# Where the depthwise convolution's taps, its tail and two sets of transposes stand in a two-layer hybrid encoder kernel

## The chip, the cores and the metric

The kernel runs on one core of a Trainium2 chip. The metric is the device time of one execution in microseconds (us). Five engines work from queues of their own, each strictly in the order of its program: PE (TensorE, matrix multiplies), DVE (VectorE), ACT (ScalarE), POOL (GpSimd) and SP, which issues the DMAs here. They wait for each other through semaphores.

## The reference, cut to what matters

Two layers are computed on x of 1 x 1024 x 1024, float32:

```python
for l in range(DEPTH):                       # 2 layers
    h = rms_norm(x, norm_mix[l]); z = h @ w_in[l]
    (q_a, k_a, v_a, q_h, i_h, f_fw, f_bw, g_h, a_c, g_c) = split(z)
    o_att = block_attention(rope(rms_norm(q_a)), rope(rms_norm(k_a)), v_a)   # 8 query, 2 key/value heads of 64
    o_hg  = hgrn2_bidirectional(q_h, i_h, f_fw, f_bw, g_h, ...)              # gated recurrence, 4 heads of 64
    u     = a_c * sigmoid(g_c)
    y     = depthwise_conv(u, w_dw) + b_dw                                   # 31 taps, 256 channels
    o_cv  = silu(layer_norm(y, ln_g, ln_b))
    x = x + concat([o_att, o_hg, o_cv]) @ w_out[l]
    x = x + square(relu(rms_norm(x) @ w_mlp_in[l])) @ w_mlp_out[l]
```

## The kernel before, in words

Channels lie on the 128 partitions and the 1024 positions on the free axis. A float32 product is made of three passes over operands split into a high and a low part (`xs`, `whi`, `wlo`), so one projection of 128 columns is 48 matmuls 128x512 at L223 (`dense_steps`), into two banks of PSUM (the tile `S2`). The projections of a layer go in a fixed order of columns: convolution inputs, the first half of the HGRN heads (`Hgrn(0)`), v, k and the four q columns, then the second half (`Hgrn(1)`). In the traces, buffer numbers are left out, so `S2` reads `S`, `x8` reads `x` and `m4` reads `m`.

What stands around the change, in the program's order, per layer:

- `conv_in(0)`, `conv_in(1)` make u for two halves of the channels. `conv(i)` is a generator: a first multiply, then 30 taps, each one DVE instruction over up to 1024 elements (L352), with a `yield` behind each. `conv_tail` is the layer norm and the swish behind both: POOL sums the halves, PE makes sums over channels (`tok_sums`, L162), ACT widens them (L168), PE flips them (`flip`, L178), DVE subtracts (L379); then squares, second sums, `rstd` (eleven small DVE steps on 128x8, L151 to L156), again widen and flip, DVE multiplies (L394), POOL scales (L397), ACT takes the sigmoid (L398), POOL multiplies (L399), and SP stores into `mixd` (L400). `cg` runs through conv(0), conv(1) and the tail.
- `Hgrn(ls)` makes five projections, evacuates each on DVE (`evac`, L322), and turns the value tile `iv` with eight PE transposes into `vt` (L442, L443).
- `h0.core()` is the recurrence of the first half: `near`, then seven levels of DVE and POOL multiplies of `X` by `T` (L525, L526), with scores on PE between (L494), masked into `A` on DVE (L501, L505). Between its steps the loop advances `qg` (the projections of v, k and q with their norms and rotations) and `cg`.
- `att_query(0)`, `keys(0)`, `h1 = Hgrn(1, ...)`: within it `mid()` computes the attention scores of units 0 and 1 (L745) ahead of the last projection, `iv`. Then `drain(cg)`, `keys(1)`, and the attention loop over 64 units: scores, P on DVE (L756), exponent on ACT (L759), its reciprocal on DVE (L760), normalisation on POOL (L761), transposes on PE (`att_flip`, L782), copies on ACT and DVE (L786, L787), values on PE (L803). The queries of units 4 to 7 are loaded by SP (L729), copied on ACT (L733) and split on DVE (L735).

The order on each engine is not the source's order. A list scheduler of the framework takes the instructions as written and starts one where it believes its inputs to be ready; a tap written late may so stand early. Tiles of a tag share a fixed number of buffers: `e` (`pse`) two banks, `c` two, `S2` two pairs, `tmp` four.

The loop and its end before:

```python
for _ in h0.core():
    for g in (qg, cg, qg, cg):
        next(g, None)
drain(qg)
while not ys[1:]:
    next(cg)
```

Of the kernel before, what the change touches and what calls it, by code (L numbers as in the profile page):

```python
# [45 lines left out]
def tile_hybrid_trunk(  # L46
# [59 lines left out]
    def tmp(shape=(P, L), dt=F32):  # L106
        return sp_.t(shape, "tmp", bufs=4, dt=dt)
# [179 lines left out]
    for l in range(DEPTH):  # L287
# [38 lines left out]
        def conv_in(i):  # L326
# [10 lines left out]
            nc.gpsimd.tensor_tensor(u, a, s, op=ALU.mult)  # L337
            us.append(u)

        def conv(i):  # L340
            u = us[i]
            y = x8()
            wof = PAR["cw"][0] + i * CK
            nc.vector.tensor_scalar(
                y, u, par[:, l, wof + CPAD : wof + CPAD + 1], pv(l, "cb", i), op0=ALU.mult, op1=ALU.add
            )
            for tap in range(CK):
                d = tap - CPAD
                if d == 0:
                    continue  # L350
                lo, hi = max(0, -d), min(L, L - d)
                nc.vector.scalar_tensor_tensor(  # L352
                    y[:, lo:hi], u[:, lo + d : hi + d], par[:, l, wof + tap : wof + tap + 1], y[:, lo:hi],
                    op0=ALU.mult, op1=ALU.add,
                )
                yield
            ys.append(y)

# [7 lines left out]
        def conv_tail(ys):  # L366
# [28 lines left out]
            for i, y in enumerate(ys):  # L395
# [3 lines left out]
                nc.gpsimd.tensor_tensor(s, s, y, op=ALU.mult)  # L399
                nc.sync.dma_start(mixd[2 + i], s)  # L400

        class Hgrn:
            def __init__(self, ls, mid=lambda: None):
                self.ls = ls

                X = self.X = hg.t([P, 4, L], "X")
                T = self.T = hg.t([P, 2, L], "T")
                vt = self.vt = hg.t([P, 8, P], "vt")
                hq = self.hq = hg.t([P, L], "m4", bufs=5)
                evac(ztile(6 + ls), hq)  # L410
                for d, kslot, qslot in ((0, 0, 2), (1, 3, 1)):
                    zt = tmp()
                    evac(ztile(10 + 2 * d + ls), zt)
                    if ls == 1:
                        next(cg, None)
                    nc.scalar.activation(T[:, d], zt, AF.Sigmoid)
                    nc.scalar.activation(X[:, kslot], zt, AF.Sigmoid, scale=-1.0)
                    om = oml[:, l, d, ls : ls + 1]
                    nc.scalar.activation(T[:, d], T[:, d], AF.Identity, scale=om, bias=lbt[:, l, d, ls : ls + 1])
                    nc.scalar.activation(X[:, kslot], X[:, kslot], AF.Copy, scale=om)  # L420
                    nc.vector.tensor_tensor(X[:, qslot], hq, T[:, d], op=ALU.mult)
                hks = self.hks = hg.t([P, L], "m4", bufs=5)
                nc.vector.tensor_tensor(hks, X[:, 0], X[:, 3], op=ALU.add)
                gl = tmp()
                evac(ztile(14 + ls), gl)
                if ls == 1:
                    next(cg, None)
                gate = tmp()
                nc.scalar.activation(gate, gl, AF.Sigmoid)
                if ls == 1:  # L430
                    nc.scalar.activation(cst.t([P, 4], "mx", bufs=4)[:, 0:1], gate[:, 0:1], AF.Exp)
                nc.gpsimd.tensor_tensor(gate, gate, gl, op=ALU.mult)
                nc.gpsimd.tensor_scalar(gate, gate, pv(l, "hn", ls), 0.0, op0=ALU.mult, op1=ALU.add)
                nc.sync.dma_start(gd[ls], gate)
                mid()
                iv = self.iv = hg.t([P, L], "m4", bufs=5)
                evac(ztile(8 + ls), iv)
                for h in range(2):
                    tpv = pse()
                    for q in range(4):  # L440
                        c = h * 4 + q
                        nc.tensor.transpose(tpv[:, q * P : (q + 1) * P], iv[:, c * P : (c + 1) * P], ident)  # L442
                    nc.scalar.activation(  # L443
                        vt[:, h * 4 : h * 4 + 4, :], tpv.rearrange("p (a b) -> p a b", a=4), AF.Copy
                    )

            def near(self):
                X, w0, iv = self.X, self.hks, self.iv
                nc.gpsimd.tensor_tensor(w0, w0, self.hq, op=ALU.mult)
                w1 = hg.t([P, L], "m4", bufs=5)  # L450
                pair = lambda t: t.rearrange("p (n h) -> p n h", h=2)
                for hf in range(2):
                    nc.vector.tensor_tensor(
                        pair(w1)[:, :, hf], pair(X[:, 1 + hf])[:, :, hf], pair(X[:, 3 - 3 * hf])[:, :, 1 - hf],
                        op=ALU.mult,
                    )
                yield
                t = tmp()
                for h in range(2):
                    sl = slice(h * 512, (h + 1) * 512)  # L460
                    d1 = pse()
                    nc.tensor.matmul(d1, same_head, w1[:, sl], start=True, stop=True)
                    for hf in range(2):
                        nc.vector.tensor_tensor(
                            pair(t[:, sl])[:, :, hf], pair(d1)[:, :, hf], pair(iv[:, sl])[:, :, 1 - hf], op=ALU.mult
                        )
                yield
                for h in range(2):
                    sl = slice(h * 512, (h + 1) * 512)
                    d0 = pse()  # L470
                    nc.tensor.matmul(d0, same_head, w0[:, sl], start=True, stop=True)
                    nc.vector.tensor_tensor(iv[:, sl], d0, iv[:, sl], op=ALU.mult)
                nc.gpsimd.tensor_tensor(iv, iv, t, op=ALU.add)
                yield

            def scores(self, lev):
                X = self.X
                s = LEVELS[lev]
                kx, qx = (hg.t([P, L], "m4", bufs=5) for _ in range(2))
                for dst, arrs in ((qx, (1, 2)), (kx, (0, 3))):  # L480
                    for hf in range(2):
                        nc.scalar.activation(
                            dst.rearrange("p (n h s) -> p n h s", h=2, s=s)[:, :, hf],
                            X[:, arrs[hf]].rearrange("p (n h s) -> p n h s", h=2, s=s)[:, :, hf],
                            AF.Copy,
                        )
                for g in range(2):
                    scs = [pse(), pse()] if g == 1 or self.ls == 1 else [psc(), psc()]
                    for q in range(4):
                        c = g * 4 + q  # L490
                        cs = slice(c * P, (c + 1) * P)
                        for hh in range(2):
                            rows = slice(64 * hh, 64 * hh + 64)
                            nc.tensor.matmul(  # L494
                                scs[hh][:, q * P : (q + 1) * P], kx[rows, cs], qx[rows, cs], start=True, stop=True
                            )
                    for hh in range(2):
                        dst = self.A[:, hh, g * 4 : g * 4 + 4, :]
                        src = scs[hh].rearrange("p (a b) -> p a b", a=4)
                        if lev == 0:  # L500
                            nc.vector.tensor_tensor(  # L501
                                dst, src, masks[:, 0].unsqueeze(1).to_broadcast([P, 4, P]), op=ALU.mult
                            )
                        else:
                            nc.vector.copy_predicated(  # L505
                                dst, masks[:, lev].unsqueeze(1).to_broadcast([P, 4, P]), src
                            )
                    yield

            def core(self):  # L510
# [3 lines left out]
                for s in (1,) + LEVELS:  # L514
# [5 lines left out]
                    for eng, d, arr, half in (  # L520
# [2 lines left out]
                        tv = Tv[:, d, :, 1 - half, 0:1].to_broadcast([P, nb, s])  # L523
                        xv = Xv[:, arr, :, half, :]
                        eng.tensor_tensor(xv, xv, tv, op=ALU.mult)  # L525
                    nc.vector.tensor_tensor(  # L526
                        Tv[:, :, :, 0, 0], Tv[:, :, :, 0, 0], Tv[:, :, :, 1, 0], op=ALU.mult
                    )
                    yield
                Tc = cst.t([P, 2, 8], "Tc", bufs=2)  # L530
                nc.vector.tensor_copy(Tc, T.rearrange("p d (n s) -> p d n s", s=P)[:, :, :, 0])
# [155 lines left out]
        def qkv():  # L687
# [5 lines left out]

            for col, part in [(5, vpart), (4, kpart)] + [(j, lambda zp, j=j: qpart(zp, j)) for j in range(4)]:
                for k, _ in enumerate(zsteps(col, lambda zp: start(part(zp)))):
                    if k == 2 and rest:
                        drain(rest.pop(0))
                    yield
            drain(rest.pop(0))

        qg = qkv()
        for _ in h0.core():
            for g in (qg, cg, qg, cg):
                next(g, None)
        drain(qg)
        while not ys[1:]:
            next(cg)

        KH, KL = [], []

# [55 lines left out]
        h1 = Hgrn(1, lambda: (att_scores(0), att_scores(1)))  # L766
        gen = h1.core()
        drain(cg)
        xsp.close()


# [513 lines left out]
```

## Time and profile before

| | |
|---|---|
| time, median of 3 runs | 2544.08 us (2543.35 to 2545.97) |
| profiled execution | 2543.87 us, its span 2541.9 us |
| PE busy | 2457.1 us, 97% |
| DVE, ACT, POOL busy | 78%, 47%, 29% |
| DVE, the 120 taps (L352) | 166.8 us, mean 1390 ns |
| chain that ended last | PE 78%, DVE 15%, ACT 3% |

The span is the time from the first to the last instruction in the trace; some 2 us of the execution lie outside of it. Layer 0's part from the convolution to the attention lies between 60 and 340 us, layer 1's between 1323 and 1600 us. A tap is written into the profile as `L352 DVE SCALAR_TENSOR_TENSOR x<-x,par,x`. A bracket behind a row of the timeline is the engine's idle time before the row and what released it.

### The profile page before, as it was taken

The page shows a single profiled execution, that of the slowest core. Times are in us where ns is not written, and L with a number is a line of the kernel's source. Part 1 is how long each engine was busy: PE and PEld are TensorE (multiplying, and loading weights), DVE is VectorE, ACT ScalarE, POOL GpSimd, SP SyncE. Part 2 cuts the span into 40 slices and gives each one's busy share as a digit, 9 for nine tenths or more (in the row PEclk, how much of TensorE's full clock was granted, in tenths as well). Part 3 has the DMA queues.
Part 4 walks back from the last instruction along what each step waited for, and adds up shares of the span by engine and source line. Part 5 has one row for each costly group of instructions (what it writes and reads, how often), then busy time and mean ns, then how long its engine had stood idle before and what let it go on. Part 6 is the DMA issues. An engine that isn't in the chain of part 4 may idle for free.

```text
span 2541.9 us, 34037 instructions
## 1 busy us (share of the span) xinstructions
PE 2457.1 (97%) x12608; PEld 2023.4 (80%) x12608; DVE 1995.0 (78%) x3051; ACT 1205.0 (47%) x1960; POOL 736.7 (29%) x463
## 2 busy tenths in 40 slices
PE   8989989999999999999999899999999999999999
PEld 7777778878788887888887777788787888878887
DVE  5998598872887778987859985898628777789876
ACT  4222478773544444443433224787635444444332
POOL 0232565433034430000123324665330354300000
PEclk9999999999999999999999999999999999999999
DMA  4101210033244448454131113000322544584542
GB/s 149 68 25 63 95 43 18 14 106 115 75 165 164 144 158 322 159 174 156 67 108 50 42 63 104 17 18 26 124 84 91 178 141 154 185 287 158 162 153 91
DMA packets 113078, 286.99 MB, mean 113 GB/s; under 512 B 11409, under 2 KB 11665, under 8 KB 112913
## 3 DMA queue, kind: packets, MB, share of 16 engines
q1 hardware_dynamic: 112912, 284.83, 32.4%
q8 instruction: 99, 1.62, 0.3%
q14 instruction: 67, 0.54, 0.1%
HBM read 197.75 MB, written 87.03 MB: 112 GB/s over the span
## 4 chain that ended last, share of the span: by engine, by line
PE 78%; DVE 15%; ACT 3%; issue 2%; POOL 2%; DMA 0%; SPq 0%; DVEq 0%; ACTq 0%; POOLq 0%
PE S L223 15%; PE S L1196 10%; PE c L995 10%; PE S L995 7%; PE e L995 7%; PE e L1196 6%; PE c L1196 6%; DVE x L352 4%; PE e L803 4%; PE c L782 3%; PE S L745 3%; PE e L494 2%; DVE P L756 1%; PE e L162 1%; PE e L583 1%
## 5 line engine op out<-in xcount | busy, mean ns | idle before, releaser
L223 PE MATMUL S<-xs,whi 128*128 128x512 f32 x1280 | 366.3, 407 | 10.6 <-ACT xs L208 9.1
L223 PEld LDWEIGHTS S<-xs,whi 128*128 128x128 f32 x1280 | 245.0, 195 | 67.5 <-ACT xs L208 9.1
L1196 PE MATMUL S<-xs,xs 128*128 128x512 f32 x816 | 201.6, 390 | 2.6 <-DVE xs L897 2.6
L223 PE MATMUL S<-xs,wlo 128*128 128x512 f32 x640 | 204.0, 399 | 0.0
L896 ACT ACTIVATE xs<-m 128x512 fp32r<-128x512 f32 x216 | 126.0, 619 | 141.6 <-DVE m L907 50.8
L761 POOL TENSOR_SCALAR P<-P,mx 128x1024 f32<-128x1024 f32 x124 | 142.6, 1150 | 164.1 <-DVE mx L760 126.2
L787 DVE TENSOR_TENSOR PT<-c,PT 128x512 fp32r<-128x512 f32 x256 | 171.1, 684 | 24.2 <-ACT PT L786 22.6
L1196 PEld LDWEIGHTS S<-xs,xs 128*128 128x128 f32 x816 | 152.8, 188 | 35.5 <-DVE xs L897 3.5
L786 ACT ACTIVATE PT<-c 128x512 fp32r<-128x512 f32 x256 | 147.5, 593 | 69.1 <-PE c L782 65.5
L199 ACT ACTIVATE whi<-raw 128x1024 fp32r<-128x1024 f32 x56 | 59.1, 1058 | 247.1 <-PE S L223 234.1
L803 PE MATMUL e<-PT,x 128*128 128x256 f32 x1024 | 172.3, 297 | 0.8 <-ACT PT L786 0.5
L756 DVE TENSOR_SCALAR_CACHE_REDUCE P<-S,nqc 128x1024 f32<-128x1024 f32 x124 | 158.5, 1278 | 14.0 <-PE S L745 8.8
L352 DVE SCALAR_TENSOR_TENSOR x<-x,par,x 128x1009 f32<-128x1009 f32 (+14 forms) x120 | 166.8, 1390 | 1.8
L782 PE MATMUL c<-cons,P 128*128 128x128 f32 x992 | 152.4, 278 | 10.5 <-POOL P L761 5.6
L897 DVE TENSOR_TENSOR xs<-m,xs 128x512 fp32r<-128x512 f32 x216 | 144.9, 694 | 22.0 <-ACT xs L896 22.0
L745 PE MATMUL S<-x,QS 128*128 128x512 f32 x480 | 154.0, 419 | 4.8 <-DVE P L756 4.5
L260 POOL TENSOR_TENSOR tmp<-tmp,tmp 128x1024 f32<-128x1024 f32 x19 | 50.6, 2662 | 360.4 <-ACT tmp L259 360.2
L759 ACT ACTIVATE P<-P,mx 128x1024 f32<-128x1024 f32 x124 | 142.4, 1149 | 24.3 <-DVE P L756 23.0
L803 PEld LDWEIGHTS e<-PT,x 128*128 128x128 f32 x1024 | 139.0, 193 | 8.5 <-ACT PT L786 2.0
L223 PEld LDWEIGHTS S<-xs,wlo 128*128 128x128 f32 x640 | 123.2, 193 | 27.1 <-issue 0.3
L782 PEld LDWEIGHTS c<-cons,P 128*128 128x128 f32 x992 | 115.3, 141 | 36.7 <-issue 10.6
L1196 PE MATMUL e<-xs,xs 128*128 128x512 f32 x552 | 140.6, 390 | 0.3 <-DVE xs L897 0.3
(310 smaller groups left out, 5639.1 us busy)
## 6 DMA issues: line engine op xcount, KB each, us to landing
m<-ad SPq DMA_DIRECT2D x104, 512.0 KB, 3.8
ad<-x SPq DMA_DIRECT2D x176, 256.0 KB, 2.2
raw<-w_in_t SPq DMA_DIRECT2D x40, 512.0 KB, 3.4
xs<-w_t SPq DMA_DIRECT2D x36, 512.0 KB, 3.7
raw<-w_t SPq DMA_DIRECT2D x36, 512.0 KB, 3.7
m<-w_t SPq DMA_DIRECT2D x32, 512.0 KB, 6.8
ad<-tmp SPq DMA_DIRECT2D x48, 256.0 KB, 2.2
x<-w_t SPq DMA_DIRECT2D x24, 512.0 KB, 4.6
```

Source lines behind the costliest of these rows:

```text
L223: nc.tensor.matmul(zp[h] if type(zp) is list else zp[:, h, :], w, xx[:, h * 512 : (h + 1) * 512], start=first, stop=last)
L352: nc.vector.scalar_tensor_tensor(y[:, lo:hi], u[:, lo + d : hi + d], par[:, l, wof + tap : wof + tap + 1], y[:, lo:hi], op0=ALU.mult, op1= ...
L745: nc.tensor.matmul(S[:, hb, :], qs, kk[:, hb * 512 : (hb + 1) * 512], start=first, stop=not first)
L756: nc.vector.tensor_scalar(Pt, S, nqc[:, j, ci : ci + 1], 3.0e38, op0=ALU.mult, op1=ALU.min, accum_out=mx[:, 1:2])
L761: nc.gpsimd.tensor_scalar(Pt, Pt, mx[:, 3:4], 0.0, op0=ALU.mult, op1=ALU.add)
L782: nc.tensor.transpose(t[:, q * P : (q + 1) * P], Pt[:, hb, q * P : (q + 1) * P], ident)
L786: nc.scalar.activation(hi, src, AF.Copy)
L787: nc.vector.tensor_tensor(lo, src, hi.bitcast(F32), op=ALU.subtract)
L803: nc.tensor.matmul(pvp[:, cs], VS[g][:, hb * 4 + kb, :], pt[:, kb, :], start=hb == 0 and n == 0, stop=hb == 1 and n == 7,)
L897: ordered("v", nc.vector.tensor_tensor(lo, src, hi.bitcast(F32), op=ALU.subtract))
L995: nc.tensor.matmul(bank, w[i][:, kt * P : (kt + 1) * P], BC[name][kt][j], start=n == 0 and name not in ("M6", "M7", "M3"), stop=n == 11, s ...
L1196: nc.tensor.matmul(banks[dt], w[i][:, dt * P : (dt + 1) * P], a[j], start=n == 0 and name not in ("M6", "M7", "M3"), stop=n == 3 * SG - 1, ...
```

## The change: what it does

1. **Taps by hand.** A helper `taps(n)` advances `cg` n steps. In `Hgrn(0)` it is called with 6, 6, 6, 6 and 5 behind the projections: 29 taps, where before none was written. In the loop of `h0.core()` one tap is written in every second step from the sixth on (12), where before two were written in every step. In `Hgrn(1)` 3, 4, 4 and 4 are written, and `drain(cg)` writes the last four taps and the whole tail behind `Hgrn(1)`. The loop that finished the taps ahead of `Hgrn(1)` is gone, so no part of the tail is written ahead of the scores of units 0 and 1 any more.
2. **A gate for the scheduler.** A tap written within the first recurrence may not be scheduled ahead of the latest masked copy (L505) or `T` product (L526): these are put into `mark`, and each tap gets an order-only dependency on the last of them. `mark` is emptied behind the recurrence and behind the tail.
3. **Two sets of transposes later.** The eight transposes of `iv` move from the end of `Hgrn` into `near`, behind its first multiplies (`turned`). In `qkv` the second part of v (its eight transposes and their split copies) is run at the seventh step of k's projection, where it was the third.

```diff
+        def after_gate(i):
+            if mark:
+                tc.add_manual_dep(i.ins, mark[-1].ins.name, mybir.DependencyInfo(
+                    mybir.DependencyClass.NoSync, mybir.DependencyReason.DATA), reason="order")
...
+        def taps(n):
+            for _ in range(n):
+                next(cg, None)
...
                 evac(ztile(6 + ls), hq)
+                taps(3 if ls else 6)
                 for d, kslot, qslot in ((0, 0, 2), (1, 3, 1)):
...
-                    if ls == 1:
-                        next(cg, None)
...
                     nc.vector.tensor_tensor(X[:, qslot], hq, T[:, d], op=ALU.mult)
+                    taps(4 if ls else 6)
...
                 evac(ztile(14 + ls), gl)
-                if ls == 1:
-                    next(cg, None)
+                taps(4 if ls else 6)
...
                 evac(ztile(8 + ls), iv)
+                if ls == 0:
+                    taps(5)
+
+            def turned(self):
                 for h in range(2):
...
                 yield
+                self.turned()
                 t = tmp()
...
-                    if k == 2 and rest:
+                    if rest and k == (6 if col == 4 else 2):
                         drain(rest.pop(0))
...
-        for _ in h0.core():
-            for g in (qg, cg, qg, cg):
-                next(g, None)
+        for n, _ in enumerate(h0.core()):
+            next(qg, None)
+            if n > 3 and n % 2:
+                taps(1)
+            next(qg, None)
         drain(qg)
-        while not ys[1:]:
-            next(cg)
+        mark.clear()
...
         drain(cg)
+        mark.clear()
```

The changed file is 17 lines longer, so its line numbers run ahead of the profile's: L400 becomes L407, L729 becomes L745, L398 becomes L405.

**DVE in the first recurrence of layer 0, at the sums for k's norm.** `nwa`, `nwy`, `nwt` are the small steps of `rstd`; rows that write `x8_200` are taps. Before:

```order
L505 COPY_PREDICATED A_129_789<-masks_15_78,c_171_1069 128x512
L352 SCALAR_TENSOR_TENSOR x8_200_1289<-x8_91_460,par_13_76,x8_200_1289 128x1014
L151 TENSOR_SCALAR nwa_173_1095<-e_172_1086 128x16
L352 SCALAR_TENSOR_TENSOR x8_200_1289<-x8_91_460,par_13_76,x8_200_1289 128x1015
L152 TENSOR_SCALAR nwy_174_1096<-nwa_173_1095 128x16
L352 SCALAR_TENSOR_TENSOR x8_200_1289<-x8_91_460,par_13_76,x8_200_1289 128x1016
L154 SCALAR_TENSOR_TENSOR nwt_175_1097<-nwy_174_1096 128x16
L352 SCALAR_TENSOR_TENSOR x8_200_1289<-x8_91_460,par_13_76,x8_200_1289 128x1017
L155 TENSOR_TENSOR nwt_175_1097<-nwt_175_1097,nwa_173_1095 128x16
```

Now, at the same place:

```order
L520 COPY_PREDICATED A_128_808<-masks_15_78,c_172_1083 128x512
L151 TENSOR_SCALAR nwa_174_1109<-e_173_1100 128x16
L152 TENSOR_SCALAR nwy_175_1110<-nwa_174_1109 128x16
L154 SCALAR_TENSOR_TENSOR nwt_176_1111<-nwy_175_1110 128x16
L155 TENSOR_TENSOR nwt_176_1111<-nwt_176_1111,nwa_174_1109 128x16
L156 SCALAR_TENSOR_TENSOR nwy_175_1110<-nwt_176_1111,nwy_175_1110 128x16
```

The taps between the small steps have moved: of the second half's 30 taps 13 stood behind the recurrence's last `T` product before, and 25 do now, the last ten of them among the evacuations of `Hgrn(1)`.

**ACT at the start of the attention, layer 0.** L398 and L405 are the tail's sigmoids, L205 splits the second key head, L733 and L749 copy the queries of units 4 to 7 (`QS_331`, `QS_329`). Before, from the tail's second widening on:

```order
L168 ACTIVATE tmp_300_2049<-nwy_298_2036 128x1024
L419 ACTIVATE T_272_1816<-T_272_1816,lbt_16_79,oml_17_80 128x1024
L420 ACTIVATE X_271_1815<-X_271_1815,oml_17_80 128x1024
L398 ACTIVATE tmp_303_2065<-x8_135_807 128x1024
L398 ACTIVATE tmp_304_2070<-x8_200_1289 128x1024
L199 ACTIVATE whi_321_2171<-raw_320_2169 128x1024
L429 ACTIVATE tmp_311_2139<-tmp_306_2082 128x1024
L431 ACT_TABLE_LOAD
L431 ACTIVATE mx_312_2141<-tmp_311_2139 128x1
L759 ACTIVATE x8_315_2152,mx_314_2151<-x8_315_2152,mx_314_2151 128x1024
```

Now, from the same widening on (the exponents of units 0 to 3 stand ahead of these rows):

```order
L168 ACTIVATE tmp_319_2199<-nwy_317_2186 128x1024
L405 ACT_TABLE_LOAD
L405 ACTIVATE tmp_322_2215<-x8_101_525 128x1024
L405 ACTIVATE tmp_323_2220<-x8_156_1000 128x1024
L457 ACTIVATE vt_272_1796<-e_357_2340 128x512
L457 ACTIVATE vt_272_1796<-e_358_2346 128x512
L205 ACTIVATE x8_326_2232<-tmp_325_2229 128x1024
L749 ACTIVATE QS_329_2239<-tmp_328_2236 128x512
L497 ACTIVATE m4_467_2862<-X_270_1794 128x128x4
L828 ACTIVATE tmp_384_2470<-e_353_2322 64x512
L829 ACTIVATE tmp_384_2470<-e_353_2322 64x512
```

The tail's sigmoids moved from ahead of the switch to the exponent's table to behind it; three rows further on stands another `L775 ACT_TABLE_LOAD`, ahead of the exponent of unit 4.

**SP at the same place.** `mixd` takes the tail's two results, `tmp<-kd` loads the second key head, `tmp<-qd` the queries of units 4 to 7 and on. Before:

```order
L400 DMA mixd_6_69<-tmp_303_2065 128x1024
L400 DMA mixd_6_69<-tmp_304_2070 128x1024
L713 DMA tmp_327_2241<-kd_9_72 64x1024
L714 DMA tmp_327_2241<-kd_9_72 64x1024
L729 DMA tmp_330_2248<-qd_8_71 64x512 x2
L434 DMA gd_10_73<-tmp_311_2139 128x1024
```

Now:

```order
L444 DMA gd_10_73<-tmp_294_2052 128x1024
L196 DMA raw_937_5219<-w_out_t 128x1024
L729 DMA tmp_325_2229<-kd_9_72 64x1024
L407 DMA mixd_6_69<-tmp_322_2215 128x1024
L407 DMA mixd_6_69<-tmp_323_2220 128x1024
L730 DMA tmp_325_2229<-kd_9_72 64x1024
L745 DMA tmp_328_2236<-qd_8_71 64x512 x2
```

The two stores of the tail still stand ahead of the query loads, and now behind the store of `gd`; one of the two key loads moved ahead of them.

More of the change, by code (lines that the diff above doesn't have):

```diff
@@ L351, in conv @@
                 lo, hi = max(0, -d), min(L, L - d)
-                nc.vector.scalar_tensor_tensor(
+                after_gate(nc.vector.scalar_tensor_tensor(
                     y[:, lo:hi], u[:, lo + d : hi + d], par[:, l, wof + tap : wof + tap + 1], y[:, lo:hi],
                     op0=ALU.mult, op1=ALU.add,
-                )
+                ))
                 yield
@@ L441, in __init__ @@
                         c = h * 4 + q
-                        nc.tensor.transpose(tpv[:, q * P : (q + 1) * P], iv[:, c * P : (c + 1) * P], ident)
+                        nc.tensor.transpose(tpv[:, q * P : (q + 1) * P], self.iv[:, c * P : (c + 1) * P], ident)
                     nc.scalar.activation(
-                        vt[:, h * 4 : h * 4 + 4, :], tpv.rearrange("p (a b) -> p a b", a=4), AF.Copy
+                        self.vt[:, h * 4 : h * 4 + 4, :], tpv.rearrange("p (a b) -> p a b", a=4), AF.Copy
                     )
@@ L504, in scores @@
                         else:
-                            nc.vector.copy_predicated(
+                            mark.append(nc.vector.copy_predicated(
                                 dst, masks[:, lev].unsqueeze(1).to_broadcast([P, 4, P]), src
-                            )
+                            ))
                     yield
@@ L525, in core @@
                         eng.tensor_tensor(xv, xv, tv, op=ALU.mult)
-                    nc.vector.tensor_tensor(
+                    mark.append(nc.vector.tensor_tensor(
                         Tv[:, :, :, 0, 0], Tv[:, :, :, 0, 0], Tv[:, :, :, 1, 0], op=ALU.mult
-                    )
+                    ))
                     yield
```

1 line of the change is left out of this document (added).

## The prediction

> **What bounds the kernel now.** I read the page first (PE 97% busy), then the busy time by stretches, TensorE's waits, the timelines of PE and DVE, and the chain that ended last. The stretches of layer 0 (columns: PE, PEld, DVE, ACT, POOL, granted clock, DMA share, GB/s):
>
> ```profile
> 69.50:118.00 48.50, 45.11 (x200) 37.01 (x198) 47.82 (x36) 14.39 (x14) 8.76 (x3) 0.99 0.16 55
> 118.00:152.00 34.00, 28.96 (x126) 21.92 (x127) 33.74 (x38) 10.68 (x19) 18.52 (x9) 0.81 0.10 32
> 172.00:202.00 30.00, 25.78 (x159) 21.02 (x159) 28.57 (x37) 9.32 (x12) 11.24 (x4) 0.94 0.15 53
> 202.00:230.00 28.00, 24.96 (x174) 20.51 (x173) 23.60 (x52) 8.08 (x12) 8.93 (x4) 0.88 0.19 66
> 262.00:316.00 54.00, 50.81 (x249) 41.69 (x249) 28.36 (x54) 24.81 (x27) 25.89 (x13) 1.00 0.26 83
> 316.00:340.00 24.00, 20.96 (x123) 15.96 (x122) 22.46 (x38) 17.01 (x29) 15.17 (x11) 1.00 0.27 89
> 340.00:400.00 60.00, 55.47 (x369) 47.87 (x368) 53.30 (x96) 46.51 (x85) 38.47 (x31) 0.97 0.08 23
> 400.00:460.00 60.00, 59.54 (x407) 51.22 (x408) 54.06 (x100) 48.57 (x87) 37.37 (x32) 1.00 0.06 19
> ```
>
> From 69.5 to 152 DVE is the full engine (81.6 of 82.5 us) and PE idles behind it; from 400 on PE is the full one, so an idle us of PE ahead of it is lost for good. PE's long waits, and what they do to its clock:
>
> ```profile
> PE e L442 <- DVE m L322: 4.3, 1, 4.3
> PE e L637 <- DVE A L501: 4.2, 1, 4.2
> PE c L539 <- ACT T L540: 3.0, 1, 3.0
> PE e L178 <- ACT tmp L168: 2.8, 1, 2.8
> ...
> 181.20 1.09 PE L178 MATMUL e<-cons,tmp 128*128 128x128 f32 x8 [1.20 <-ACT tmp L168]
> 182.05 1.17 PE L223 MATMUL S<-xs,whi 128*128 128x512 f32 x4
> ...
> 191.18 2.17 PE L494 MATMUL e<-m,m 64*128 64x128 f32 x16 [2.05 <-DVE tmp L660]
> 193.27 2.07 PE L223 MATMUL S<-xs,whi 128*128 128x512 f32 x4
> ```
>
> After 1.20 us of idling four matmuls take 1.17 us; after 2.05 us they take 2.07, half speed.
>
> **What the change can win, ahead of the attention.** Idle PE in the first five stretches is 3.39 + 5.04 + 4.22 + 3.04 + 3.19 = 18.9 us, and the clock costs 0.01 x 48.5 + 0.19 x 34 + 0.06 x 30 + 0.12 x 28 = 12.2 us: 31 us per layer at most. DVE's rows there:
>
> ```profile
> 107.10 10.59 DVE L352 SCALAR_TENSOR_TENSOR x<-x,par,x 128x1017 f32<-128x1017 f32 x6
> 117.61 1.22 DVE L322 TENSOR_TENSOR m<-S,Rb 128x1024 f32<-128x1024 f32 x1
> 107.22 3.41 POOL L432 TENSOR_TENSOR tmp<-tmp,tmp 128x1024 f32<-128x1024 f32 x1 [4.70 <-ACT tmp L429]
> 135.62 1.26 DVE L352 SCALAR_TENSOR_TENSOR x<-x,par,x 128x1010 f32<-128x1010 f32 x1
> ```
>
> - The wait for `iv` (4.3 us): six taps still stand ahead of its evacuation, and POOL's L432 still stretches them (six at 1.2 us would be 7.1, not 10.6). The evacuation stays near 117 us; the later transposes only let five more matmuls (1.1 us) pass first. I keep a wait of 2 to 3 us.
> - The wait at v's transposes (4.2 us): two taps fewer ahead of the masks (2.4 us of DVE), and some 18 matmuls (4.1 us) and one score pair more ahead of the transposes. It goes. Late next are the score banks: two taps now stand ahead of v's split copies, which free the banks of the next scores: about 2 us, new.
> - k's norm: no tap between the small steps. Its wait of 1.2 shrinks to under 1; the wait for L660 behind it (2.05) stays, since it hangs on the rotation's POOL multiply.
> - L539 (3.0): the last `T` product now comes well ahead, so it goes; the 2.8 us at L178 go too, if the taps beside that `rstd` don't push it, for which I keep up to 2.
>
> What stays is about 10 us of idling and 5 of slow clock, so the win is 31 - 15 = 16, less about 1 for the norm behind the taps: 15 us per layer. Bounds: 8 (only v's and L539's waits go, with their clock) and 25 (nothing over 1.2 us stays). The taps themselves cost nothing more: 60 per layer before and after, and DVE has 25 us free in 262 to 316.
>
> **What it costs, at the attention's start.** The tail now begins where `iv`'s projection ends (316.6 before; call it E), since its first flips stand behind that projection on PE. What hangs on the tail is shown in layer 1's chain, where it ended last already:
>
> ```profile
> 1561.16 4.39 POOL x L397 x2
> 1567.87 2.40 POOL m L449
> 1572.66 0.33 SPq L400
> 1573.58 4.57 DMA tmp<-kd
> 1578.22 1.07 ACT x L205
> 1581.89 2.71 DVE QS L735
> ...
> SPq L400 <- POOL tmp L399: 16.5, 2, 12.2
> ```
>
> SP waits for the tail's products ahead of its stores, and behind these wait the second key head and the queries of units 4 to 7; their scores cannot start before. That order on SP stays, and the tail moves back. Its pieces, in layer 0:
>
> ```profile
> 280.72 1.03 PE L178 MATMUL e<-cons,tmp 128*128 128x128 f32 x8
> 289.09 1.84 PE L162 MATMUL e<-cons,tmp 128*128 128x1 f32 x16
> 290.97 0.17 DVE L151 TENSOR_SCALAR nwa<-e 128x8 f32<-128x8 f32 x1 [0.45 <-PE e L162]
> 294.03 0.17 DVE L156 SCALAR_TENSOR_TENSOR nwy<-nwt,nwy 128x8 f32<-128x8 f32 x1
> 295.35 1.09 PE L178 MATMUL e<-cons,tmp 128*128 128x128 f32 x8
> 304.96 5.05 SPq L400 DMA_DIRECT2D mixd<-tmp  x2
> 305.57 1.28 ACT L431 ACT_TABLE_LOAD   x1
> 306.86 0.20 ACT L431 ACTIVATE mx<-tmp 128x1 f32<-128x1 f32 x1
> 323.11 0.47 PE L745 MATMUL S<-x,QS 128*128 128x512 f32 x1 [0.69 <-DVE P L756]
> 335.05 0.60 PE L782 MATMUL c<-cons,P 128*128 128x128 f32 x4
> ```
>
> The steps of one attention unit, from the costliest groups:
>
> ```profile
> L756 DVE TENSOR_SCALAR_CACHE_REDUCE P<-S,nqc 128x1024 f32<-128x1024 f32 x124 | 158.5, 1278 | 14.0 <-PE S L745 8.8
> L759 ACT ACTIVATE P<-P,mx 128x1024 f32<-128x1024 f32 x124 | 142.4, 1149 | 24.3 <-DVE P L756 23.0
> L761 POOL TENSOR_SCALAR P<-P,mx 128x1024 f32<-128x1024 f32 x124 | 142.6, 1150 | 164.1 <-DVE mx L760 126.2
> ```
>
> 1. First flips to the end of the second sums: 280.72 to 290.93, 10 us. So E + 10.
> 2. `rstd`: 3.2 us when alone (290.97 to 294.20). Now eleven big DVE instructions of units 0 to 3 and of the recurrence stand between its steps, the last two waiting for unit 3's transposes. Bounds 3 and 12; by the order it is nearer the upper one: 9. E + 19.
> 3. Widening and its place behind three ACT copies: 2 us. Second flips at E + 21.
> 4. Flips to the stores: 295.35 to 310.0 is 14.7 us, less POOL's L449 between (2.4), plus a `T` product and two `X` multiplies that DVE now does first (1 to 3). I take 13.5: E + 34. The sigmoids' own table load (1.28) passes while ACT waits for POOL.
> 5. Stores to unit 4's scores: 310.0 to 323.1 is 13.1 us, less an evacuation, a weight split and some waiting of DVE for POOL; 7.5 to 11, I take 9. E + 43.
> 6. To unit 4's transposes: scores 1.1, row minimum 1.3, table load 1.28, exponent 1.15, reciprocal, normalising 1.15: 6. E + 49, where before it was 335.05, E + 18.5.
>
> PE's work in that stretch is two flips and second sums 3.4, scores of units 2 and 3 2.2, eight groups of P transposes 3.5, 32 value matmuls 4.2, `iv`'s transposes and the first of `near` 2.2, then five scores 5.5 and 1.3: 22 us. So 27 us idle, against 3.0 before in 316 to 340: 24 lost, of which I give back 2 of the 4.5 us idle in 340 to 400, whose ramp is then over. Cost 22 us per layer. Bounds: 15 (`rstd` alone, 7.5 after the stores) and 30 (all upper ends). SP stores and loads are as many as before; its weight loads move a few places and land long before their use.
>
> The Trainium skill ("ScalarE: Activation LUTs", What ACT_TABLE_LOAD costs) gives a table switch 1.28 us for the load and 1.38 for a drain, 2.66 together; the row has 1.28 with the next activation right behind it, so the drain isn't seen here. With it, one switch per layer on the path, the sum below would be 2 x 1.4 us higher.
>
> **Sum.** Both layers have the same rows. 2 x (22 - 15) = +14 us on the profiled 2543.87 (the median of the runs, 2544.08, is 0.2 higher): 2558 us.
>
> **Rivals.**
>
> - *The recurrence wins more than the tail costs (faster).* DVE, relieved of the taps in the first recurrence, keeps every PE wait there under 1.2 us and so the clock whole. Worth 27 of the 31 us; against 22 it gives -5 per layer, 2534. It decides once the win passes the cost by 2.6 us per layer. For it: DVE is full in just those stretches. Against it: six taps still stand ahead of `iv` and two ahead of v's copies.
> - *They cancel.* The three waits that I keep, near 2 us each, are too short to slow the clock, as the 1.20 us one is; the win is 20 and the sum 2 x 2: 2548. For it 181.20, against it 193.27. The Trainium skill ("TensorE: Matmul & The Clock Gate", Part 1: The HAM clock gate) says that the clock halves after an idle window of about 3.4 us, by a free-running window; by that rule waits of 2 us would mostly cost no clock, and the row at 193.27 speaks against it.
> - *The taps don't leave the path (slower by more).* DVE stays full to the end of the first recurrence, only v's and L539's waits go, and the win is 8: 2 x 14, 2572. For it: DVE has as much to do. Against it: 25 of the last 30 taps stand behind the last `T` product, where DVE is free.
>
> **How the numbers follow.** The main case has 0.5, the faster rival 0.2, cancelling 0.15, the third 0.15. The likeliest is 2558, by itself 2549 to 2570. The range 2534 to 2580 takes in the rivals; beyond it lie the joint ends of the bounds, -10 and +22 us per layer. Measurement tells 0.2%, 5 us, from no change: slower has 0.5 + 0.15 and loses a little to the cancelling case, 0.64; same 0.15; faster 0.21.
>
> **What would show it.** Right: the stretch from 118 to 152 with a clock above 0.9 and no wait of L637's successor; PE reaching the end of `iv`'s projection some 18 us earlier; then over 20 us of idle PE ahead of unit 4's scores, ACT waiting for POOL at the sigmoids and SP at the tail's stores, and table loads before and after. Wrong: if the scores of unit 4 start within 30 us of E, the cost is under 10 us and the kernel is faster; or if PE idles as before at 118 and 146, the win is gone.

## The result, and the profile after

| | before | after |
|---|---|---|
| time, median of 6 runs | 2543.61 us (2540.46 to 2545.97) | 2591.74 us (2590.61 to 2592.72) |
| ratio | | 1.0189, 95% interval 1.0179 to 1.0199 |
| profiled execution, its span | 2543.87, 2541.9 | 2592.72, 2590.6 |
| PE busy, granted clock | 97%, 0.985 | 95%, 0.978 |

The kernel became 48 us slower, 24 per layer, where the prediction had 7. The stretches of layer 0 after the change, with the columns of the prediction (busy time of PE, PEld, DVE, ACT, POOL, then granted clock, DMA share, GB/s); 152 to 172 and 309 to 360 are added:

```profile
69.50:118.00 48.50, 45.10 (x199) 37.02 (x198) 47.90 (x36) 13.69 (x13) 8.68 (x3) 1.00 0.16 55
118.00:152.00 34.00, 30.60 (x156) 22.59 (x156) 32.47 (x37) 10.60 (x20) 17.79 (x9) 0.95 0.10 32
152.00:172.00 20.00, 17.38 (x100) 14.02 (x101) 14.26 (x28) 5.14 (x8) 7.22 (x4) 0.91 0.08 27
172.00:202.00 30.00, 29.97 (x207) 24.13 (x207) 28.62 (x45) 10.84 (x15) 11.93 (x6) 1.00 0.21 79
202.00:230.00 28.00, 25.11 (x184) 20.94 (x184) 26.30 (x58) 5.08 (x8) 3.87 (x2) 0.94 0.15 57
262.00:316.00 54.00, 46.74 (x210) 37.90 (x208) 24.72 (x34) 24.39 (x27) 18.72 (x10) 0.94 0.17 60
309.00:360.00 51.00, 32.30 (x143) 24.45 (x141) 36.53 (x60) 27.11 (x39) 26.45 (x16) 0.70 0.20 63
340.00:400.00 60.00, 47.05 (x254) 36.55 (x252) 40.14 (x71) 37.28 (x65) 30.15 (x23) 0.86 0.16 49
400.00:460.00 60.00, 59.71 (x412) 50.98 (x410) 52.67 (x100) 46.25 (x85) 33.04 (x29) 1.00 0.07 19
```

The stretch from 118 to 152 gained (30.6 us busy at 0.95, where it was 28.96 at 0.81). The loss lies from 262 to 400: in 309 to 360, from the end of `iv`'s projection to unit 4's transposes, PE idles 18.7 us and works at 0.70 of its clock in the rest.

TensorE's waits, layer 0 (in all us, times, longest):

```profile
PE S L761 <- DVE P L772: 5.8, 2, 4.3
PE e L178 <- ACT tmp L168: 5.0, 2, 3.3
PE e L456 <- DVE m L322: 4.7, 1, 4.7
PE S L761 <- DVE QS L751: 4.4, 1, 4.4
...
PE e L162 <- POOL tmp L375: 2.9, 1, 2.9
PE e L509 <- DVE ms L693: 2.9, 1, 2.9
PE e L509 <- DVE tmp L675: 2.3, 1, 2.3
...
PE e L509 <- DVE x L657: 1.5, 1, 1.5
```

The waits at v's transposes and at the recurrence's last product (4.2 and 3.0 us before) are gone. That for `iv` is as long as ever, and the recurrence's scores (L509) wait in three places for DVE. New are the waits for the tail's first sums (L162), at its flips (L178, 3.3 of the 5.0 us) and for the queries of unit 4. The chain that ended last, from the last part of `iv`'s projection on (start, us, what), and SP's wait for the tail's products:

```profile
299.63 9.48 PE S L223 x39
...
317.18 3.01 PE e L162 x16
...
330.23 1.15 DVE T L541
...
334.52 1.28 DVE x L401 x2
...
339.13 4.70 POOL tmp L406 x2
344.23 3.96 DMA tmp<-kd
348.28 1.06 ACT x L205
...
350.96 0.70 DVE QS L751
351.70 3.80 PE S L761 x8
SPq L407 <- POOL tmp L406: 22.7, 2, 20.8
```

`iv`'s projection ends at 299.63 + 9.48 = 309.1, which is E. From there this is the chain that the prediction wrote down, nearly to the microsecond: `rstd` done at E + 21 (19 predicted), stores at E + 35 (34), unit 4's scores at E + 42.6 (43).

For the experiments each layer is cut at four landmarks, read from the timelines of PE and DVE: its first projection matmul, the evacuation of `Hgrn(1)`'s `iv`, unit 4's first scores, the first matmul of the MLP. The us between them, layer 0 / layer 1, each from one profiled execution:

| kernel | start to `iv` | to unit 4 | to the MLP |
|---|---|---|---|
| before | 309.7 / 305.5 | 4.3 / 5.4 | 329.1 / 329.1 |
| after | 301.9 / 296.3 | 42.1 / 41.5 | 325.2 / 325.9 |
| e1 tail early | 301.1 / 302.0 | 5.4 / 5.4 | 333.1 / 331.2 |
| e2 tail late alone | 301.7 / 299.8 | 45.7 / 45.8 | 325.6 / 324.9 |
| e4 no gate | 311.3 / 308.0 | 42.4 / 42.2 | 324.4 / 324.5 |
| e6c second key head late | 299.2 / 296.3 | 35.1 / 35.1 | 318.6 / 318.9 |
| f2 half the tail late | 305.0 / 300.5 | 23.6 / 23.6 | 321.1 / 322.5 |
| f4 gate at `iv` | 309.2 / 306.8 | 5.3 / 5.4 | 332.1 / 333.4 |
| g3 gate alone | 333.2 / 330.5 | 5.4 / 5.4 | 327.1 / 327.0 |

Runs of one kernel differ by up to 10 us (f1: 2532.7 to 2542.9; e1: 2536.8 to 2545.8), so a difference of 2 or 3 us in a cell says little by itself.

### The profile page after: what moved, and what is told of

It is laid out like the page before. It is cut to its first block, busy times and chain, and to the rows that moved or that the text cites. A ratio compares the mean times of both kernels' runs of the same rounds, so it can differ in the third digit from the quotient of the medians.

```text
span 2590.6 us, 34050 instructions
## 1 busy us (share of the span) xinstructions
PE 2473.0 (95%) x12608; PEld 2031.3 (78%) x12608; DVE 1993.8 (77%) x3051; ACT 1206.9 (47%) x1964; POOL 722.0 (28%) x463
## 4 chain that ended last, share of the span: by engine, by line
PE 77%; DVE 14%; issue 3%; ACT 2%; POOL 2%; DMA 1%; SPq 0%; DVEq 0%; POOLq 0%; ACTq 0%
PE S L223 14%; PE S L1213 10%; PE c L1012 9%; PE e L1213 7%; PE e L1012 6%; PE c L1213 6%; PE S L1012 6%; DVE x L359 4%; PE c L799 4%; PE S L761 4%; PE e L820 4%; PE e L509 3%; DVE P L772 1%; PE e L598 1%; PE e L162 1%
## 5 line engine op out<-in xcount | busy, mean ns | idle before, releaser
L772 DVE TENSOR_SCALAR_CACHE_REDUCE P<-S,nqc 128x1024 f32<-128x1024 f32 x124 | 158.7, 1280 | 27.4 <-PE S L761 17.5
L761 PE MATMUL S<-x,QS 128*128 128x512 f32 x480 | 154.1, 430 | 23.5 <-DVE P L772 13.6
L775 ACT ACTIVATE P<-P,mx 128x1024 f32<-128x1024 f32 x124 | 142.4, 1149 | 34.9 <-DVE P L772 22.7
```

Of the source, the lines that this page charges most:

```text
L761: nc.tensor.matmul(S[:, hb, :], qs, kk[:, hb * 512 : (hb + 1) * 512], start=first, stop=not first)
L772: nc.vector.tensor_scalar(Pt, S, nqc[:, j, ci : ci + 1], 3.0e38, op0=ALU.mult, op1=ALU.min, accum_out=mx[:, 1:2])
L775: nc.scalar.activation(Pt, Pt, AF.Exp, bias=mx[:, 1:2], scale=-1.0, accum_out=mx[:, 2:3])
```

## Experiments: which part of the change costs

**e1, tail early.** The changed kernel with the tail's place undone:

```diff
-                taps(3 if ls else 6)
+                taps(0 if ls else 6)
...
                     evac(ztile(10 + 2 * d + ls), zt)
+                    taps(ls)
...
-                    taps(4 if ls else 6)
+                    taps(0 if ls else 6)
...
-                taps(4 if ls else 6)
+                taps(1 if ls else 6)
...
         drain(qg)
+        while not ys[1:]:
+            next(cg)
         mark.clear()
```

> The changed kernel with the tail where it was before: all taps written ahead of Hgrn(1), the tail's three steps within it. Theory A (the tail's late place costs all of it and more, the placing of the taps wins some 8 us per layer, as the second half's first evacuation, 263.0 before and 255.0 after, says): 2543.6 - 16 = 2528 us, unit 4's scores at some 315 us. Theory B (the placing of the taps wins nothing once the tail stands early again, since the taps are then too late for the tail): within 5 us of 2544. Theory C (the tail is only half of the loss): above 2555.

Measured: 2542.08 us, before 2542.8; ratio 0.9998 (0.9987 to 1.0008). The loss is gone, as A says, but A's win is not there either: B's time. In its one profiled execution `iv` comes 8.6 and 3.5 us sooner than before, and 5.1 and 2.1 us of it are lost behind (table, second and third columns), in layer 0 from this wait on:

```profile
315.38 0.93 PE L764 MATMUL S<-x,QS 128*128 128x512 f32 x3 [2.97 <-DVE P L775]
```

**e2, tail late alone.** The kernel before without the two `next(cg, None)` in `Hgrn(1)`, of which one stands in a loop, so that the tail's three steps go.

> The kernel before with the tail alone moved: its three steps are no longer written within Hgrn(1), so drain(cg) writes them behind it; taps and transposes as before. Theory A (from the end of iv's projection, E, the way to unit 4's scores is 42.6 us as in the changed kernel, 6.5 before; E itself some 4 us earlier, 4 us given back later): +28 per layer, 2600 us. The prediction's own size of the cost (22 per layer): 2588 us. Theory C (half of the loss lies with the taps): below 2575.

Measured: 2601.66 us, ratio 1.0236 (1.0219 to 1.0252): +58.9, 29.4 per layer. Theory A, to 2 us. The tail's place costs more than the whole change does; the rest of the change gives 10 us back (12 by the two ratios), not 30.

**e3, flips back.** The changed kernel with `turned` at the end of `Hgrn` and `k == 2` for all columns.

> The changed kernel with both sets of transposes where they were before. Theory A (the loss lies at the tail; the later transposes save v's wait of 4.2 us and little else): 2592 + 2 x 3 = 2598 us, between 2592 and 2602. Rival (the later transposes push the recurrence back and so cost): below 2588.

Measured: 2587.43 us, ratio 1.0185 (1.0164 to 1.0206), the changed kernel's 1.0189: no difference that can be told. It is not that nothing moves: in e3's one profiled execution, its fastest (2583.2 us), `iv` comes 9.3 and 6.7 us sooner than in the changed kernel, and some 4 us of it are lost again on the way to unit 4.

**e5, tail early and flips back**: e1 and e3 together.

> The changed kernel with the tail early, as in e1, and both sets of transposes where they were before, so that of the change only the placing of the taps and the gate are left. If the later transposes cost something (e3 was 4 us under the changed kernel, at the edge of its interval): 2538 us. If they save v's wait and nothing gives it back: 2548 us. If they do nothing: 2542, as e1.

Measured: 2543.89 us, ratio 1.0000 (0.9991 to 1.0009). With either place of the tail the later transposes change the time by nothing that can be told.

**e4, no gate.** The changed kernel with `after_gate` doing nothing.

> The changed kernel without the gate: taps written in the recurrence may be scheduled ahead of the masked copies and T products; places as written stay. Theory A (the gate keeps taps out of k's norm and so makes the 7.5 us won by k's evacuation at 152.4): 2592 + 2 x 6 = 2604 us, k's norm with taps between its small steps. Rival (the gate only leaves DVE idle, 5.7 us from 152 to 172): 2592 - 2 x 4 = 2584 us.

Measured: 2613.07 us, ratio 1.0281 (1.0261 to 1.0300). With the late tail the gate is worth 21 us (23 by the two ratios), and theory A's direction holds, at nearly twice its size: in layer 0 five taps stand again between the small steps of k's norm, k's evacuation comes at 162.50 us instead of 152.38, and `iv` comes 9 to 12 us later (table).

## Experiments: what holds unit 4

**e6c, second key head late.** `keys(1)` moves from ahead of the attention loop to its unit 8, and SP then issues the queries of units 4 to 7 ahead of the tail's stores:

```diff
-        keys(1)
...
         for u in range(NU):
+            if u == 8:
+                keys(1)
```

> The changed kernel with only the second key head's load moved to unit 8; SP then issues the queries of units 4 to 7 ahead of the tail's stores. Theory D1 (SP's order is what holds unit 4): its scores come right behind the tail's last multiplies on DVE, at E + 30 where they were at E + 42.6: 2592 - 24 = 2568 us. Rival D2 (DVE itself waits: the recurrence's products at L479 stand ahead of the split of the queries and need a tmp buffer that only the tail's store sets free): unit 4 at E + 37, 2592 - 11 = 2581 us.

Measured: 2566.07 us, ratio 1.0091 (1.0076 to 1.0106): 26 us of the 48 gone, the time that D1 gave. But unit 4 starts at E + 35, near D2's place: 7 us sooner, and 13 per layer are gained, since the wait of the next scores for P (L761, 5.8 us) is gone too. The stretch of layer 0 now, and DVE at the split of unit 4's queries (L751):

```profile
309.00:360.00 51.00, 34.35 (x173) 26.79 (x172) 41.49 (x70) 30.99 (x48) 34.33 (x20) 0.80 0.21 63
360.00:372.00 12.00, 12.00 (x83) 10.15 (x82) 11.19 (x20) 9.14 (x17) 7.25 (x7) 1.00 0.06 22
...
342.15 0.42 DVE L479 TENSOR_TENSOR tmp<-e,m 128x256 f32<-128x256 f32 x1 [5.53 <-PE e L477]
342.61 0.69 DVE L751 TENSOR_TENSOR QS<-tmp,QS 64x512 fp32r<-64x512 f32 x1
```

In the changed kernel PE was busy for 5.99 of the 12 us from 360 to 372 (its row stands further below). In e6c SP issues the query loads at 318.75 us, 21 us ahead of the tail's stores, and still unit 4 starts only at 343.35: ACT copies the queries at 340.83, behind the tail's sigmoids, and on DVE the recurrence's product L479 stands ahead of their split, as D2 had it, but waits for PE and not for the tail's store. So moving the key load gives back half of the loss. SP's order is the likely cause of that half, not the only one possible: the edit also takes the key head's copy (1.06 us on ACT) and split (1.23 us on DVE) from ahead of the queries.

**e6, query first**: `att_query(1)` ahead of `drain(cg)`, with an `x8` tile. **e6b**: the same, with `keys(1)` at unit 8.

> The changed kernel, but the queries of units 4 to 7 are loaded, copied and split ahead of drain(cg) (into a tile x8), so that SP, ACT and DVE have them ahead of the tail; the tail is as late as in the changed kernel. Theory D (the late tail costs only because the attention's next queries stand behind it on the in-order queues): units 4 to 7 run beside the tail, some 20 us of PE work per layer, then the queries of units 8 on still wait for the tail's stores: 12 us per layer regained, 2568 us (2556 to 2572). Rival E (the tail's small steps and the recurrence's products on DVE bind that stretch whatever is loaded): above 2582.

> As e6, and the second key head, which only unit 32 needs, is loaded at unit 8. Theory D: the queries of units 8 on now come right behind the stores, 4 us (one load) sooner: 3 to 4 us per layer under e6, some 2561 us. Rival E: as e6.

Measured: 2567.41 us, ratio 1.0088 (1.0071 to 1.0105), and 2566.61, 1.0091 (1.0072 to 1.0109). Theory D for e6; that the key load costs another 3 to 4 us per layer there falls. Three ways of getting the queries past the tail end within 1.4 us of each other, so what remains, 23 us, is hardly loading. In e6's layer 0 PE's waits for split queries come to 3.3 us between 300 and 420 (1.8 for `QS`, below, and 1.5 for units 4 to 7, split in the `x8` tile); the rest is many short waits beside the tail's steps, with the clock at 0.80 in 309 to 360:

```profile
PE S L766 <- POOL QS L756: 1.8, 1, 1.8
```

**f2, half the tail late.** e1 with `taps(ls if d == 0 else 0)` and none behind the gate's column: the first half of the tail early, the second half late.

> e1 with only the first half of the tail (sums, subtraction, squares) written within Hgrn(1); the second half (second sums, rstd, multiplies, sigmoids, stores) behind it, as in the changed kernel. Theory A (the cost is the length of what is left of the chain behind E): rstd now runs beside the scores of units 0 and 1, the last multiplies follow iv's evacuation, the stores come at E + 13 to 15 and unit 4 at E + 21 to 23, where the changed kernel has 42 and e1 5: 16 us per layer more than e1, less 2 that the earlier E gives: 2542 + 28 = 2570 us (2562 to 2576). Rival (what costs is any tail behind E, since SP, ACT and POOL then meet the attention): above 2580.

Measured: 2556.27 us, ratio 1.0050 (1.0037 to 1.0063). Unit 4 starts 23.6 us behind `iv`, as forecast, but that costs 14 us and not 28: the way from there to the MLP is 9 to 12 us shorter than in e1 (table), so PE has done other work in the meantime. PE still stands 9.2 us, behind products on DVE that are longer beside POOL's multiplies (two `X` products took 1.28 us and the `T` product 1.22 in the changed kernel, at 145.44 and 330.15):

```profile
PE c L802 <- DVE mx L779: 9.2, 1, 9.2
321.77 5.56 POOL L406 TENSOR_TENSOR tmp<-tmp,x 128x1024 f32<-128x1024 f32 x2
321.59 3.53 DVE L541 TENSOR_TENSOR X<-X,T 128x512 f32<-128x512 f32 x2
325.05 3.37 DVE L542 TENSOR_TENSOR T<-T 128x1024 f32<-128x1024 f32 x1
```

**f1, tail early and second key head late.** e1 with e6c's edit.

> e1 (tail early, taps and transposes as changed) with the second key head loaded at unit 8. In e1 the row minima of units 2 and 3 stand on DVE behind the split of that key head and PE waits 3.0 us for them, after which the clock is 0.86 in 316 to 340. Theory F (that split is the cause): 3 us per layer less, 2536 us. Rival (the wait then goes to the evacuation of iv and the split of the queries, which stand there too): 2542, as e1.

Measured: 2539.31 us, ratio 0.9982 (0.9973 to 0.9990): 4.6 us under the kernel before, the only version with all its work done whose interval lies under the kernel before. Its mechanism is not shown: against e1 it is 2.8 us, the intervals overlap, and a wait of 2.7 us for the row minima is still there.

**f3**: the kernel before with e6c's edit alone.

> The kernel before with only the second key head's load moved to unit 8. There PE waited 1.85 and 0.69 us at that place, in layer 0: 2 us per layer at most, 2540 us. Rival (it is hidden): 2543.

Measured: 2542.17 us, ratio 0.9995 (0.9986 to 1.0004): hidden, the rival.

## Experiments: where the win ahead of the attention went

**g1, no taps.** The kernel before with its 120 taps left out.

> The kernel before with all 120 taps left out (each half of the convolution keeps its first multiply; the tail then begins within the recurrence): the most that any placing of the taps could win. If all idling and slow clock ahead of the attention in the kernel before is due to the taps (31 us per layer, as the prediction summed it): 2544 - 62 = 2482 us. If the other chains there (norms, rotations, the recurrence itself) hold half of it: 2512. If the taps were nearly hidden, and a placing has little to win: above 2528.

Measured: 2516.99 us, ratio 0.9899 (0.9882 to 0.9915). Leaving out all taps saves 26.4 us, 13.2 per layer: near the middle case, and less than the 15 that the prediction expected from moving them. What idles without them:

```profile
118.00:152.00 34.00, 31.38 (x168) 23.58 (x167) 23.43 (x42) 14.68 (x21) 18.14 (x12) 0.95 0.18 62
...
172.00:202.00 30.00, 26.96 (x163) 21.31 (x163) 22.97 (x40) 10.72 (x15) 8.54 (x6) 0.89 0.17 62
PE e L494 <- DVE x L642: 2.5, 1, 2.5
PE e L494 <- DVE tmp L660: 2.4, 1, 2.4
```

The scores still wait for v's split copies and for the rotation, although DVE is free for 10 of the 34 us.

**f4, gate at `iv`.** f1 with the taps behind the gate's column written behind `iv`, and held behind its evacuation:

```diff
-                taps(1 if ls else 6)
+                taps(1)
...
-                evac(ztile(8 + ls), iv)
+                last = evac(ztile(8 + ls), iv)
                 if ls == 0:
-                    taps(5)
+                    mark.append(last)
+                    taps(10)
```

> f1 with another use of the gate: in Hgrn(0) one tap instead of six behind the last evacuation but one, ten behind that of iv, and these may not be scheduled ahead of it. It takes away the wait for iv (4.73 us in the changed kernel, where the prediction kept 2 to 3). Theory G (that wait and the slow clock behind it are lost for good): 5 us per layer less than f1. Rival H (DVE has as many taps to do before the recurrence ends, so the wait moves to v's transposes and the scores behind them): the same as f1, within 3 us.

Measured: 2550.89 us, ratio 1.0028 (1.0018 to 1.0038): 11.6 us slower than f1. G falls, and H was too kind. The wait for `iv` is gone; f4's stretches and f1's (of each kernel the two ahead of 152 and their sum):

```profile
69.50:118.00 48.50, 47.17 (x213) 38.87 (x212) 36.90 (x32) 14.76 (x15) 8.45 (x5) 1.00 0.16 55
118.00:152.00 34.00, 28.14 (x148) 20.98 (x149) 33.40 (x38) 9.04 (x17) 18.52 (x8) 0.96 0.09 32
sum 82.50, PE 75.32 PEld 59.85 DVE 70.30 ACT 23.81 POOL 26.97; mean PE 37.66 PEld 29.93 DVE 35.15 ACT 11.90 POOL 13.48
...
69.50:118.00 48.50, 44.77 (x198) 36.74 (x196) 47.90 (x37) 13.68 (x13) 8.66 (x3) 1.00 0.15 55
118.00:152.00 34.00, 30.47 (x157) 22.90 (x157) 32.46 (x37) 10.93 (x20) 17.80 (x9) 0.95 0.09 32
sum 82.50, PE 75.24 PEld 59.65 DVE 80.36 ACT 24.61 POOL 26.46; mean PE 37.62 PEld 29.82 DVE 40.18 ACT 12.31 POOL 13.23
```

PE was busy for the same time by 152 in both, 75.3 and 75.2 us: what it won ahead of 118 it lost behind. DVE idled for 11.6 of the 48.5 us ahead of 118 in f4, and its taps were still to do. The 11.6 us of the whole lie behind 152: there f4's clock is lower, 0.90, 0.89 and 0.94 in 152 to 172, 172 to 202 and 202 to 230, where f1 has 0.95, 0.92 and 1.00.

**g2, tail early without the gate**: f1 with `after_gate` doing nothing. **g3, gate alone**: the kernel before with `after_gate` and `mark`.

> f1 (tail early, second key head late) without the gate: taps written in the recurrence may go ahead of its masked copies and T products again. With the late tail the gate was worth 21 us (e4 against the changed kernel). If it is worth as much here: 2539 + 21 = 2560 us. If it only mattered because the taps without it made the tail later still: within 5 us of 2539.

> The kernel before with the gate alone: same places in the source, two taps written in each step of the recurrence, none scheduled ahead of the copy or product before it. The taps then spread over the recurrence and stand between the small steps of k's norm and of the q norms. If the win lies in keeping taps off the evacuations ahead of iv (three taps there, where nine stood): 2544 - 2 x 4 = 2536 us. If taps between the norm's steps cost more than that: slower, 2550 to 2560 us.

Measured: g2 2550.20 us, ratio 1.0028 (1.0017 to 1.0040); g3 2590.35, 1.0183 (1.0165 to 1.0202). With the tail early the gate is worth 11 us, about half of what it is with the late tail, between the two forecasts. Without the new places it costs 47: held back out of the projections, the taps fill the norms and the scores, and between 60 and 300 us PE waits longest for the states and the masks:

```profile
PE e L590 <- DVE m L565: 8.2, 2, 6.0
PE e L644 <- DVE A L508: 5.2, 1, 5.2
PE e L162 <- DVE nwt L155: 2.8, 1, 2.8
```

The 29 taps written early and the gate are one tool: each without the other is worse than neither.

## Why the prediction was right and wrong

**Right: slower, and for the reason given.** The tail's place alone costs 58.9 us (e2), undoing it removes the loss (e1). The steps of the chain were each within 3 us. For one step of the cost's mechanism, SP's stores ahead of the queries, e6c speaks, with the reservation above.

**Right: single waits.** v's and L539's waits went, k's evacuation came 7.5 us sooner (159.88 before, 152.38 after), the rotation's wait stayed (2.3, kept at 2.05), a new one of 1.5 us (2 forecast) stands behind v's split copies, and the one at L178 went from 2.8 to 1.7 us (up to 2 kept).

**The step that failed: "the win is 31 - 15 = 16, less about 1 ... 15 us per layer", with bounds 8 and 25.** Measured against e2, the rest of the change wins 9.9 us by the medians and 12 by the two ratios, 5 to 6 per layer, under the lower bound (the two intervals together allow some 3.5 to 8.5); with the tail early it wins nothing that can be told (e1, e5). Of the 34 us by which 2558 fell short, the win makes about 2 x (15 - 5) = 20 and the cost about 2 x (29.4 - 22) = 15. Two errors made the win's size:

- The 31 us (their clock part adds up to 12.1, not 12.2) were taken as DVE's debt to the taps. Without any tap 10.6 us of idling stay in 69.5 to 316 (246.5 less 235.9 busy) and, worked out as the prediction did, about 5 of slow clock. This is just what the prediction "kept", so it forecast a placing as good as no taps; g1 puts the ceiling near 13.2, below the term.
- A wait that goes was counted as won. On a stretch in which DVE is full it can simply move: f4 shows that for `iv`. That the new waits of 2.9 and 1.5 us at L509 are v's and L539's, moved, is likely but not shown. The wait for `iv`, kept at 2 to 3 us, was 4.7.

In the changed kernel a third thing ate into it, which had no term: the tail's first sums, written behind the scores of units 0 and 1, stand on POOL behind a weight split, and PE waits for them in the midst of the projections:

```profile
288.64 2.38 POOL L200 TENSOR_TENSOR wlo<-raw,whi 128x1024 fp32r<-128x1024 f32 x1 [2.29 <-ACT whi L199]
290.97 2.34 POOL L375 TENSOR_TENSOR tmp<-x,x 128x1024 f32<-128x1024 f32 x1
...
293.37 3.07 PE L162 MATMUL e<-cons,tmp 128*128 128x1 f32 x16 [2.94 <-POOL tmp L375]
296.30 2.06 PE L223 MATMUL S<-xs,whi 128*128 128x512 f32 x4
```

So E came 7.5 us sooner (316.6 before, 309.1 after), where some 18 were forecast.

**The other term: cost 22 per layer, 29.4 measured, inside the bounds of 15 and 30 at their upper end.** From E to unit 4's transposes 27 us of idling were forecast, and nothing for the clock; 18.7 of idling and 0.30 x 32.3 = 9.7 of slow clock came, 28.4 in all. The sum is right by luck: the clock's missing term and the idling that was too long cancel. Wrong in the sum was the 2 us given back behind it, out of the 4.5 of idling in 340 to 400 before. In 360 to 400 PE now lost 6.0 us by idling and 0.12 x 6.0 + 0.07 x 28.0 = 2.7 by the clock, since a row minimum (L772, at 369.51) stands on DVE behind a `T` product that waits for POOL, and PE waits 4.3 us for it with its next scores:

```profile
360.00:372.00 12.00, 5.99 (x32) 4.53 (x33) 6.28 (x13) 5.89 (x11) 9.83 (x7) 0.88 0.07 22
372.00:400.00 28.00, 28.00 (x182) 24.14 (x180) 22.98 (x42) 20.64 (x39) 12.48 (x11) 0.93 0.03 10
368.90 0.62 DVE L541 TENSOR_TENSOR T<-T 128x256 f32<-128x256 f32 x1 [4.80 <-POOL X L540]
```

**The rivals.** "The taps don't leave the path", win 8 and 2572 us, came nearest, and its reason, DVE having as much to do, is what f4 shows; its win was still too large. "The recurrence wins more", which needs 27 us per layer, and "They cancel", which needs 20, are both out of reach if g1's 13.2 is the ceiling.

## What to carry to other kernels

Before a stall is booked as a win, run the kernel without the work that is blamed for it: what idles then is held by something else, and the difference is an estimate of the ceiling for any new place. Where another engine than the idling one is full, a removed wait can move to the next place as long as that engine's work stays (f4), and leaving it idle to clear one wait costs time later. A long chain through five engines is best placed where the bound engine has other work (58.9 us in e2); behind that, a store that waits in SP's order holds the loads written after it.

## What the runs showed of the hardware

- After a wait of 2.94 us the sixteen small sums took 3.07 us, where they took 1.84 before, and the four matmuls at 296.30 2.06, where four take 1.07; the matmuls at 299.00 still took 1.91. The granted clock is 0.50 from 296.3 to 300.7 and 1.00 from 304. So the half speed outlasted the wait by some 7 us of busy work. The Trainium skill ("TensorE: Matmul & The Clock Gate", Part 1: The HAM clock gate) puts the way back to full speed at one or more busy windows of about 3.4 us; here it took about twice 3.4.
- The recurrence's 128x1024 `T` product on DVE took 1.22 us in the changed kernel (its 1.15 at 330.23 in the chain) and 3.37 beside POOL's two-input multiplies (f2, 325.05). The Trainium skill ("GPSIMD Engine Reference", 1. Specifications) names two SBUF inputs on DVE as a case of contention with GpSimd; the trace agrees, and its price here is a factor of 2.8.
- An order-only dependency on tap instructions moved the time by -21, -11 and +47 us in three settings (e4, g2, g3).
